# A seven-product block multiplication on TensorE: a new order of the products, a held queue of adding transfers, and operands in pieces of 512

## The chip, the cores and the metric

The kernel runs on one core of one Trainium2 chip. A core has TensorE (matrix products, written to the eight banks of PSUM), VectorE, ScalarE, GpSimd and SyncE, each with an instruction stream of its own that runs in order, and 16 DMA engines that all transfers share. In the profile these are PE, DVE, ACT, POOL and SP. The metric is the device time of one execution in microseconds (us), less being better.

## The reference, cut to what matters

One layer of a decoder trunk on 512 positions of 2048 channels, in float32:

```python
h = rmsnorm(x, norm_g)
proj = h @ w_in                      # 2048 x 15360
a_u, a_b, a_c, a_z, b_v, b_g, b_z, c_u, c_z, gates = split(proj)
y_a = short_conv_mixer(a_u, a_b, a_c, a_z, ...)      # 3 taps, then @ w_br_a
y_b = conformer_conv_mixer(b_v, b_g, b_z, ...)       # 31 taps, layer norm, then @ w_br_b
y_c = pool_mixer(c_u, c_z, ...)                      # causal means, then @ w_br_c
g = sigmoid(gates)                                    # 3 x 2048
merged = g0 * y_a + g1 * y_b + g2 * y_c
out = rmsnorm(x + merged @ w_o, final_g)
```

The change lies in the projection `h @ w_in`, 15360 columns wide.

## The kernel before, in words

**Units and products.** The projection is done in 15 units of 1024 columns (two column blocks of 512, "left" and "right"). In each unit the input x is cut into a 2 by 2 grid (256 positions by 1024 channels each), the weights into a 2 by 2 grid (1024 channels by 512 columns), and the block product is formed by seven products instead of eight, by sums and differences of the blocks (a Winograd form of Strassen's scheme). The seven are named in `PRODUCTS` (L58): 11, 12, s1, s4, s2, s3, 22. Each runs over 8 slices of 128 channels, in 4 steps of two slices.

**Halves.** Every operand of float32 is split in a high part (a cast by ACT) and a low part (a subtraction by DVE). A product takes three matmuls per slice and bank: high x high (L433), low x high (L434), high x low (L435). So a product is 8 slices x 2 banks x 3 = 48 matmuls of 512 columns, a unit 336.

**Weights.** `Weights` (L92) runs a list of stages, four per product (28 per unit). A stage's raw weights lie in a tile of 128x1024: rawA (4 buffers) or rawB (6). "load" is a transfer from SP's queue (L113); "add" is a transfer from POOL's queue that adds a second block to what lies in the tile (L119); "sum" is an addition on DVE of the tile that another product holds (L134). `split_to` (L144) then makes `wh` on ACT (L155) and `wl` on DVE (L156) in 3 buffers each, two stages ahead of the product. An add may start only when the split before it has read the tile.

**Banks.** In `unit` (L422) 11 is written to two banks X, 12 to two banks V, s1 to two banks Z, s4 into Z on top, s2 into X on top, s3 into X, 22 into X. Between two products into the same banks, their contents are copied out by ACT (`snap`, L441) or added to an earlier copy by DVE (`join`, L446), and the next product's first matmul must wait for that. `on11` to `on22` finish the four quarters (gates, SiLU and so on); in the first unit they are put off into the second one (`delayed`), since the norm's factor is not known yet.

**The first unit** also makes the seven operands of x, which stay for all later units: `make` (L365) scales by the norm's gain (`gcol`), forms sums and differences (`less`, L357) and splits them in halves (`operand`, L344, and `quarter`, L349). x11, x12, x22, x21 are read by SP's queue (L228), interleaved with the first weights.

**What sets the order.** Engine streams are laid down by a scheduler ahead of time, from the program's order and priorities; on the chip each stream runs in order. Between the matmuls `feed` hands out a list of side tasks (convolution taps, pooling, norms) at half a unit of cost per slice. After the units come three branch products and the output product, which the change doesn't touch.

Of the kernel before, what the change touches and what calls it, by code (L numbers as in the profile page):

```python
# [8 lines left out]
F32 = mybir.dt.float32  # L9
# [37 lines left out]
for _c in (0, CH):  # L47
# [8 lines left out]

PRODUCTS = (
    ("11", "A", "load", 0, 0),  # L58
    ("12", "B", "load", 1, 0),
    ("s1", "A", "add", 0, 1),  # L60
    ("s4", "B", "load", 1, 1),
    ("s2", "A", "sum", 1, 1),
    ("s3", "B", "add", 0, 1),
    ("22", "A", "add", 1, 0),
)
STEPS = KD // 4
# [13 lines left out]
def stages():  # L80

    out = []
    for u in range(len(UNITS)):
        for name, tag, what, row, col in PRODUCTS:
            key = (u, tag, name == "12")
            out += [(tag, key + (s,), what, block(u, row, col, s)) for s in range(STEPS)]
# [5 lines left out]
class Weights:  # L92
# [3 lines left out]
    def __init__(self, tc, nc, pools, parts, src, load_ahead, split_ahead):  # L96
# [4 lines left out]
        self.first_sum = {s[3]: n for n, s in enumerate(self.stages) if s[2] == "sum"}  # L101
        self.raw, self.raw_of, self.held, self.done = {}, {}, {}, {}
        self.loaded = self.summed = self.split = self.at = 0

    def load_to(self, n):
        while self.loaded < min(n, len(self.stages)):
            tag, key, what, b = self.stages[self.loaded]
            if what == "sum":
                pass
            elif what == "load":  # L110
                t = self.pools[tag].tile([P, RAW], F32, tag=tag, name=f"raw{tag}{self.loaded}")
                for at in self.pieces(self.loaded):
                    self.nc.sync.dma_start(out=t[:, at], in_=self.src[b][:, at])  # L113
            else:
                t, before = self.raw[key]
                assert self.split > before
                first = self.first_sum.get(self.raw_of[key], -1)
                assert first < self.summed
                self.nc.gpsimd.dma_start(out=t, in_=self.src[b], accum_op=ALU.add)  # L119
            if what == "load":  # L120
                self.raw_of[key] = b
                self.held[b] = t
            if what != "sum":
                self.raw[key] = t, self.loaded
            self.loaded += 1

    def sum_to(self, n):
        while self.summed < min(n, len(self.stages)):
            _, key, what, b = self.stages[self.summed]
            if what == "sum":  # L130
                t, before = self.raw[key]
                assert self.split > before and self.loaded > self.summed
                with self.tc.high_priority(AHEAD):
                    self.nc.vector.tensor_tensor(out=t, in0=t, in1=self.held[b], op=ALU.add)  # L134
                self.raw[key] = t, self.summed
# [908 lines left out]
```

## Time and profile before

| | |
|---|---|
| Median of 3 runs | 1708.18 us (1707.02 to 1710.57) |
| The profiled execution's own time | 1707.05 us |
| Its span (first to last instruction) | 1705.3 us |
| DVE busy | 1140.5 us (67%) |
| ACT busy | 736.4 us (43%) |
| Matmuls | 7332, weight loads for them 7332 |
| First product starts | 7.10 us |
| HBM read, written | 277.00 MB, 35.65 MB |

Busy time is the time in which an engine executes; a share that is high over the span says little of a stage. The profile names, for each idle stretch of an engine, what ended it ("PE X L433 <- DVE snap L446": the matmul into X on L433 waited for DVE's `join`). A matmul of 512 columns is listed with some 0.39 us, since its end is modelled; back to back they start every 0.23 us, so short delays show only in their starts.

### The profile page before, as it was taken

How to read it: one execution, taken by the hardware profiler on the slowest of the kernel's cores; microseconds unless marked ns; L12 is line 12 of the kernel's file. 1: busy time of each engine (PE TensorE's matmuls, PEld its weight loads, DVE VectorE, ACT ScalarE, POOL GpSimd, SP SyncE). 2: the span in 40 equal slices, each digit the busy share in tenths (PEclk: the TensorE clock that was granted, in tenths of full speed). 3: DMA queues.
4: the chain of work that ended last, by engine and by line, in shares of the span. 5: the costliest groups of instructions: out<-in, count | busy, mean ns of one | idle time of the engine just before them, and what ended most of it. 6: DMA issues, size and time to landing. Idle time of an engine off the chain costs nothing.

```text
span 1705.3 us, 19733 instructions
## 1 busy us (share of the span) xinstructions
PE 1651.0 (97%) x7332; PEld 1348.6 (79%) x7332; DVE 1140.5 (67%) x1420; ACT 736.4 (43%) x919; POOL 156.9 (9%) x186
## 2 busy tenths in 40 slices
PE   7899999999999999999999989999999999999997
PEld 5677877877878787888878868888888888888887
DVE  5946699799869969967786866555743444453342
ACT  5645543434344454546544544445631211222222
POOL 1101010101011111111111111110100000000000
PEclk9999999999999999999999999999999999999999
DMA  9686867667585877688979887868994544443202
GB/s 309 141 242 140 232 140 193 143 179 168 153 181 142 196 189 171 181 217 262 267 206 251 244 237 168 225 158 240 255 314 153 181 144 148 136 136 100 91 34 99
DMA packets 110864, 313.95 MB, mean 184 GB/s; under 512 B 12208, under 2 KB 16432, under 8 KB 110768
## 3 DMA queue, kind: packets, MB, share of 16 engines
q1 hardware_dynamic: 63392, 179.50, 31.7%
q0 software_dynamic: 25920, 94.38, 30.5%
q10 hardware_dynamic: 21456, 38.82, 6.2%
q8 instruction: 57, 0.93, 0.2%
q14 instruction: 39, 0.32, 0.1%
HBM read 277.00 MB, written 35.65 MB: 183 GB/s over the span
## 4 chain that ended last, share of the span: by engine, by line
PE 84%; DVE 6%; issue 2%; ACT 1%; DMA 1%; ACTq 0%; SPq 0%; DVEq 0%
PE X L433 11%; PE X L434 11%; PE X L435 11%; PE Z L433 5%; PE Z L435 5%; PE y L872 5%; PE y L870 5%; PE y L871 5%; PE Z L434 5%; PE o L944 3%; PE o L946 3%; PE o L945 3%; DVE wl L156 2%; PE V L433 2%; PE V L434 2%; PE V L435 2%
## 5 line engine op out<-in xcount | busy, mean ns | idle before, releaser
L156 DVE TENSOR_TENSOR wl<-rawA,wh 128x1024 fp32r<-128x1024 f32 (+1 forms) x281 | 342.1, 1219 | 219.2 <-ACT wh L155 216.6
L155 ACT CAST wh<-rawA 128x1024 fp32r<-128x1024 f32 (+1 forms) x281 | 294.5, 1050 | 448.6 <-PE X L434 133.3
L156 DVE TENSOR_TENSOR wl<-rawB,wh 128x1024 fp32r<-128x1024 f32 x220 | 268.4, 1223 | 256.3 <-ACT wh L155 256.2
L155 ACT CAST wh<-rawB 128x1024 fp32r<-128x1024 f32 x220 | 231.4, 1053 | 348.5 <-PE X L434 103.7
L433 PE MATMUL X<-wh,x 128*128 128x512 f32 x480 | 188.4, 395 | 17.7 <-DVE snap L446 14.8
L433 PE MATMUL Z<-wh,xs 128*128 128x512 f32 x480 | 188.8, 396 | 5.5 <-ACT snap L441 4.1
L433 PE MATMUL X<-wh,xs 128*128 128x512 f32 x480 | 189.3, 395 | 1.9 <-ACT xs L346 1.7
L434 PE MATMUL Z<-wh,xs 128*128 128x512 f32 x480 | 188.5, 393 | 2.0 <-DVE xs L347 2.0
L434 PE MATMUL X<-wh,x 128*128 128x512 f32 x480 | 188.2, 392 | 0.1
L434 PE MATMUL X<-wh,xs 128*128 128x512 f32 x480 | 187.5, 391 | 0.0
L435 PE MATMUL X<-wl,xs 128*128 128x512 f32 x480 | 174.1, 391 | 6.4 <-DVE wl L156 6.3
L435 PE MATMUL Z<-wl,xs 128*128 128x512 f32 x480 | 175.1, 395 | 5.1 <-DVE wl L156 5.1
L435 PE MATMUL X<-wl,x 128*128 128x512 f32 x480 | 177.5, 394 | 0.0
L556 DVE SCALAR_TENSOR_TENSOR conv<-v,prm,conv 128x485 f32<-128x485 f32 (+14 forms) x240 | 167.4, 732 | 0.1
L119 POOL DMA_DIRECT2D rawA<-wts x120 | 104.1, 868 | 567.0 <-DVE wl L156 553.3
L870 PE MATMUL y<-wh,u 128*128 128x512 f32 x384 | 149.9, 390 | 0.0
L871 PE MATMUL y<-wh,u 128*128 128x512 f32 x384 | 149.7, 390 | 0.0
L872 PE MATMUL y<-wl,u 128*128 128x512 f32 x384 | 149.5, 390 | 0.0
L433 PEld LDWEIGHTS X<-wh,x 128*128 128x128 f32 x480 | 90.4, 189 | 42.0 <-issue 10.2
L433 PEld LDWEIGHTS Z<-wh,xs 128*128 128x128 f32 x480 | 90.7, 189 | 30.8 <-ACT snap L441 10.2
L433 PEld LDWEIGHTS X<-wh,xs 128*128 128x128 f32 x480 | 90.3, 188 | 27.7 <-ACT snap L441 6.3
L435 PEld LDWEIGHTS Z<-wl,xs 128*128 128x128 f32 x480 | 90.1, 189 | 27.7 <-DVE wl L156 9.2
(173 smaller groups left out, 2360.2 us busy)
## 6 DMA issues: line engine op xcount, KB each, us to landing
rawB<-wts SPq DMA_DIRECT2D x160, 512.0 KB, 5.2
rawA<-wts POOLq DMA_DIRECT2D x120, 512.0 KB, 8.1
rawA<-wts SPq DMA_DIRECT2D x99, 512.0 KB, 4.2
rawB<-wts POOLq DMA_DIRECT2D x60, 512.0 KB, 6.0
g<-g SPq DMA_DIRECT2D x48, 256.0 KB, 4.3
d<-turn ACTq DMA_DIRECT2D x32, 256.0 KB, 7.7
g<-gate ACTq DMA_DIRECT2D x24, 256.0 KB, 4.1
g<-snap ACTq DMA_DIRECT2D x24, 256.0 KB, 5.4
```

Of the source, the lines that this page charges most:

```text
L119: self.nc.gpsimd.dma_start(out=t, in_=self.src[b], accum_op=ALU.add)
L155: self.nc.scalar.copy(out=h[:, at], in_=raw[:, at])
L156: self.nc.vector.tensor_tensor(out=l[:, at], in0=raw[:, at], in1=h[:, at].bitcast(F32), op=ALU.subtract)
L433: T.matmul(p, lhsT=xh, rhs=h, start=start and k == 0, stop=False, skip_group_check=True)
L434: T.matmul(p, lhsT=xl, rhs=h, start=False, stop=False, skip_group_check=True)
L435: T.matmul(p, lhsT=xh, rhs=l, start=False, stop=k == KB - 1, skip_group_check=True)
L556: V.scalar_tensor_tensor(out=c[:, s:], in0=v[:, : S - s], scalar=pcol(P_BW, i * CONV_B + CONV_B - 1 - s), in1=c[:, s:], op0=ALU.mult, op1= ...
L870: T.matmul(banks[t], lhsT=uh[:, tk], rhs=h, start=k == 0, stop=False)
L871: T.matmul(banks[t], lhsT=ul[:, tk], rhs=h, start=False, stop=False)
L872: T.matmul(banks[t], lhsT=uh[:, tk], rhs=l, start=False, stop=k == KB - 1)
L944: T.matmul(pt[t], lhsT=mh[:, tk], rhs=h, start=k == 0, stop=False)
L945: T.matmul(pt[t], lhsT=ml[:, tk], rhs=h, start=False, stop=False)
```

## The change

- The products' order in every unit but the first becomes 11, s1, s2, s4, s3, 12, 22, so that between two products into the same pair of banks there is one into another pair. Since s2's sum needs the block of s4 before s4 runs, that block is loaded earlier.
- In the first unit the order is 11, 12, s1, s2, s4, s3, 22, and s2's weights come by an adding transfer in place of the DVE sum.
- The transfers are planned ahead as a list of events. An add is issued one stage after the split that frees it at the earliest; s1 and s3 now follow their predecessor in the tile (11 and s4) by four stages, where it was eight.
- POOL gets a copy of one column, `hold`, which reads the last block of x12; POOL's later transfers stand behind it.
- The operands: scaling by ACT in two pieces of 256 in place, then the cast and the subtraction on 512 at once; sums and differences on 512 too. `ngcol` goes.

```diff
 PRODUCTS = (
     ("11", "A", "load", 0, 0),
+    ("s1", "A", "add", 0, 1),
+    ("s2", "A", "sum", 1, 1),
+    ("s4", "B", "load", 1, 1),
+    ("s3", "B", "add", 0, 1),
     ("12", "B", "load", 1, 0),
...
     ("22", "A", "add", 1, 0),
 )
+FIRST = (PRODUCTS[0], PRODUCTS[5], PRODUCTS[1], ("s2", "A", "add", 1, 1), *PRODUCTS[3:5], PRODUCTS[6])
...
+        for n, (_, key, what, b) in enumerate(self.stages):
             if what == "load":
-                self.raw_of[key] = b
-                self.held[b] = t
+                out.append((min(need[b], n) - self.load_ahead, n))
+            elif what == "add":
+                out.append((max(n - self.load_ahead, before[key] + 1), n))
+            before[key] = n
+        return sorted(out)
...
+    def transfer(self):
+        n = self.events.popleft()[1]
+        tag, key, what, b = self.stages[n]
+        if what == "load":
+            t = self.raw[key] = self.held[b] = self.pools[tag].tile([P, RAW], F32, tag=tag, name=f"raw{tag}{n}")
+            for at in self.pieces(n):
+                self.nc.sync.dma_start(out=t[:, at], in_=self.src[b][:, at])
+        else:
+            self.nc.gpsimd.dma_start(out=self.raw[key], in_=self.src[b], accum_op=ALU.add)
...
-            self.load_to(n_stage + 1)
-            self.sum_to(n_stage + 3)
-            self.load_to(n_stage + 1 + self.load_ahead)
+            self.sum_to(n_stage + 2)
+            while self.events and self.events[0][0] <= n_stage:
+                self.transfer()
...
     for j in range(STEPS):
-        w.load_to(STEPS + j + 1)
+        w.transfer()
         xload(nc.sync, x12[j], j, 1, 0)
+    hold = const.tile([P, 1], F32, name="hold")
+    nc.gpsimd.tensor_copy(out=hold, in_=x12[STEPS - 1][:, 1, HT - 1 :])
...
-    def quarter(name, j, src, rows):
-        t = sets[name][j] = slot(F32R, f"x{name}")
+    def scale(src, j, rows):
+
         for c in range(2):
-            g = gcol[:, KB * rows + 2 * j + c :][:, :1]
-            h, l = t[:, c, half[0]], t[:, c, half[1]]
-            A.activation(out=h, in_=src[:, c], func=AF.Copy, scale=g)
-            V.scalar_tensor_tensor(
-                out=l, in0=src[:, c], scalar=g, in1=h.bitcast(F32), op0=ALU.mult, op1=ALU.subtract
-            )
...
+            A.activation(out=src[:, c], in_=src[:, c], func=AF.Copy, scale=gcol[:, KB * rows + 2 * j + c :][:, :1])
+
+    def less(out, in0, in1, sign=None):
+
+        if sign is None:
+            V.tensor_tensor(out=out, in0=in0, in1=in1, op=ALU.subtract)
+        else:
+            V.scalar_tensor_tensor(out=out, in0=in0, scalar=sign, in1=in1, op0=ALU.mult, op1=ALU.subtract)
...
         if name == "11":
-            quarter(name, j, x11, 0)
+            scale(x11, j, 0)
+            operand(name, j, x11)
         elif name == "12":
-            quarter(name, j, x12[j], 1)
+            scale(x12[j], j, 1)
+            operand(name, j, x12[j])
         elif name == "s1":
...
-            less(qs[j], x22[j], x21, j, 1, gcol)
+            scale(x21, j, 0)
+            scale(x22[j], j, 1)
+            less(qs[j], x22[j], x21)
+            operand(name, j, qs[j])
+        elif name == "s2":
+            less(qs[j], x11, qs[j], -1.0)
             operand(name, j, qs[j])
         elif name == "s4":
-            less(qs[j], x11, qs[j], j, 0, ngcol)
-            less(x12[j], x12[j], qs[j], j, 1, ngcol)
-            operand(name, j, x12[j])
-        elif name == "s2":
+            less(qs[j], qs[j], x12[j], -1.0)
             operand(name, j, qs[j])
...
         X = [psum("X") for _ in range(2)]
         run("11", X, True)
         a = snap(X)
-        U = [psum("V") for _ in range(2)]
-        run("12", U, True)
-        join(U, a, on11)
+        if first:
+            second()
         Z = [psum("Z") for _ in range(2)]
         run("s1", Z, True)
         e = snap(Z)
-        run("s4", Z, False)
         run("s2", X, False)
         u = snap(X)
+        run("s4", Z, False)
         join(Z, u, on12)
         run("s3", X, False)
         join(X, e, lambda i, t: on22(i + 2, t))
+        if not first:
+            second()
         run("22", X, False)
```

The new `second()` runs 12 and joins its banks. In `multiplied` the product of the left and right quarter is now formed when both are there, since 12 may come last.

PE's stream in the second unit, before: the last matmuls of s3 and the first of 22, all into the banks X_870 and X_871.

```order
L433 MATMUL X_871<-wh_1300,xs_60_704 128x512
L434 MATMUL X_871<-wh_1300,xs_60_704 128x512
L435 MATMUL X_871<-wl_1301,xs_60_704 128x512
L433 MATMUL X_870<-wh_1318,x_61_724 128x512
L434 MATMUL X_870<-wh_1318,x_61_724 128x512
```

PE's stream in the second unit of the changed kernel, where s3 (into X_851 and X_852) ends and 12 (into V_1264 and V_1265) begins.

```order
L434 MATMUL X_852<-wh_1210,xs_60_696 128x512
L435 MATMUL X_852<-wh_1210,xs_60_696 128x512
L436 MATMUL X_852<-wl_1211,xs_60_696 128x512
L434 MATMUL V_1264<-wh_1227,x_21_233 128x512
L435 MATMUL V_1264<-wh_1227,x_21_233 128x512
L434 MATMUL V_1265<-wh_1227,x_21_233 128x512
```

48 matmuls of product 12 now stand between s3 and 22; in the same way s2 stands between s1 and s4, and s4 between s2 and s3. In the first unit s3 and 22 still follow each other.

POOL's stream at the start, before: the adds of s1 (onto 11's tiles rawA_93 to rawA_103), then those of s3.

```order
L242 AFFINE_SELECT ident<-ident 128x128
L119 DMA rawA_93<-wts 128x1024
L119 DMA rawA_97<-wts 128x1024
L119 DMA rawA_100<-wts 128x1024
L119 DMA rawA_103<-wts 128x1024
L119 DMA rawB_334<-wts 128x1024
```

POOL's stream at the start of the changed kernel; x_8_88 is the last block of x12.

```order
L249 AFFINE_SELECT ident<-ident 128x128
L132 DMA rawA_93<-wts 128x1024
L132 DMA rawA_97<-wts 128x1024
L132 DMA rawA_100<-wts 128x1024
L132 DMA rawA_103<-wts 128x1024
L242 COPY hold<-x_8_88 128x1
L132 DMA rawA_93<-wts 128x1024
```

The copy stands behind the four adds of s1 and ahead of the adds of s2, which are new.

ACT's stream in the first unit, before: from the split of s1's first weights (wh_336) to the first operand of s1 (xs_30_331).

```order
L155 CAST wh_336<-rawA_93 128x1024
L376 ACTIVATE xa_81<-xa_81,gcol 128x256
L155 CAST wh_362<-rawA_97 128x1024
L376 ACTIVATE xa_81<-xa_81,gcol 128x256
L376 ACTIVATE xa_82<-xa_82,gcol 128x256 x2
L155 CAST wh_392<-rawA_100 128x1024
L346 CAST xs_30_331<-q_326 128x2x256
```

The same stretch of the changed kernel (wh_337 to xs_30_332; x_9 to x_11 are blocks of x22, x_28_306 is the last operand of 12).

```order
L160 CAST wh_337<-rawA_93 128x1024
L357 ACTIVATE x_9_89<-x_9_89,gcol 128x256 x2
L351 CAST x_28_306<-x_8_88 128x2x256
L357 ACTIVATE xa_81<-xa_81,gcol 128x256 x2
L357 ACTIVATE x_10_90<-x_10_90,gcol 128x256 x2
L357 ACTIVATE xa_82<-xa_82,gcol 128x256 x2
L357 ACTIVATE x_11_91<-x_11_91,gcol 128x256
L160 CAST wh_365<-rawA_97 128x1024
L357 ACTIVATE x_11_91<-x_11_91,gcol 128x256
L351 CAST xs_30_332<-q_326 128x2x256
```

Ahead of the first operand of s1 stand the scalings of x22 and a cast for 12, which were not there; one weight cast (of rawA_100) moved behind it.

## Rows read from the trace of the kernel before

**Rows 1.** The page: span, and busy time of each engine.

```profile
span 1705.3 us, 19733 instructions
PE 1651.0 (97%) x7332; PEld 1348.6 (79%) x7332; DVE 1140.5 (67%) x1420; ACT 736.4 (43%) x919; POOL 156.9 (9%) x186
```

**Rows 2.** PE's waits from 100 to 1290 us: in total, times, longest.

```profile
PE X L433 <- DVE snap L446: 12.4, 13, 2.4
PE X L435 <- DVE wl L156: 6.3, 2, 4.2
...
PE Z L433 <- ACT snap L441: 3.1, 3, 1.4
```

**Rows 3.** PE's timeline, 11 to 12: start, duration, engine, line, operation, tiles.

```profile
1109.26 0.39 PE L435 MATMUL X<-wl,x 128*128 128x512 f32 x1
1109.49 0.39 PE L433 MATMUL V<-wh,x 128*128 128x512 f32 x1
```

**Rows 4.** PE's timeline where s1 ends and s4 begins in the same banks.

```profile
1131.02 0.39 PE L435 MATMUL Z<-wl,xs 128*128 128x512 f32 x1
1131.41 0.50 PE L433 MATMUL Z<-wh,xs 128*128 128x512 f32 x1
1131.75 0.40 PE L434 MATMUL Z<-wh,xs 128*128 128x512 f32 x1
```

**Rows 5.** Units: length, busy PE, PEld, DVE, ACT, POOL; PEclk, DMA share, GB/s.

```profile
343.87:425.46 81.59, 79.42 (x353) 64.34 (x353) 81.59 (x104) 33.59 (x36) 10.38 (x12) 1.00 0.70 171
506.96:589.22 82.26, 80.50 (x353) 65.68 (x353) 80.13 (x101) 36.21 (x41) 10.41 (x12) 0.98 0.69 167
753.37:835.50 82.13, 81.93 (x372) 66.78 (x373) 61.09 (x66) 50.29 (x65) 10.38 (x12) 1.00 0.93 258
1087.65:1164.91 77.26, 77.07 (x336) 62.82 (x337) 42.71 (x39) 37.44 (x43) 10.42 (x12) 1.00 0.77 191
```

**Rows 6.** PE's timeline in the first unit: 12's first matmuls and 22's first.

```profile
25.66 1.22 PE L433 MATMUL V<-wh,x 128*128 128x512 f32 x2 [5.78 <-ACT x L354]
...
98.72 0.47 PE L433 MATMUL X<-wh,x 128*128 128x512 f32 x1 [2.32 <-DVE snap L446]
```

**Rows 7.** Stretches of 5 us in the first unit, columns as in rows 5.

```profile
20.00:25.00 5.00, 0.00 (x0) 0.00 (x0) 1.23 (x1) 1.04 (x1) 0.00 (x0) 0.76 1.05 254
...
45.00:50.00 5.00, 5.00 (x20) 4.07 (x19) 5.00 (x11) 2.09 (x3) 0.00 (x0) 0.85 0.41 151
...
75.00:80.00 5.00, 5.00 (x24) 4.14 (x23) 5.00 (x10) 3.23 (x5) 1.73 (x2) 1.00 0.77 129
```

**Rows 8.** DVE's timeline in the first unit.

```profile
44.26 1.67 DVE L362 SCALAR_TENSOR_TENSOR q<-xa,ngcol,q 128x256 f32<-128x256 f32 x4
...
46.44 1.22 DVE L134 TENSOR_TENSOR rawA<-rawA,rawB 128x1024 f32<-128x1024 f32 x1
47.58 0.48 DVE L362 SCALAR_TENSOR_TENSOR x<-x,ngcol,q 128x256 f32<-128x256 f32 x1
...
68.73 2.50 DVE L347 TENSOR_TENSOR xs<-q,xs 128x512 fp32r<-128x512 f32 x4
```

**Rows 9.** ACT's timeline in the first unit.

```profile
20.09 1.04 ACT L155 CAST wh<-rawB 128x1024 fp32r<-128x1024 f32 x1 [2.96 <-DMA rawB<-wts]
25.10 0.91 ACT L354 ACTIVATE x<-x,gcol 128x256 fp32r<-128x256 f32 x2 [3.96 <-DMA x<-xT]
...
39.39 0.61 ACT L346 CAST xs<-q 128x512 fp32r<-128x512 f32 x1
39.91 0.91 ACT L376 ACTIVATE xa<-xa,gcol 128x256 f32<-128x256 f32 x2
```

**Rows 10.** POOL's timeline: the first adds of s1 in the first and in a later unit.

```profile
6.48 1.01 POOL L119 DMA_DIRECT2D rawA<-wts  x1 [5.10 <-DVE wl L156]
...
1095.75 0.86 POOL L119 DMA_DIRECT2D rawA<-wts  x1 [24.39 <-DVE wl L156]
```

**Rows 11.** The adding transfers of L119: issue to landing.

```profile
DMA to landing us min/median/max: 5.3/7.1/12.7
```

**Rows 12.** The page's DMA queues: packets, MB, share of 16 engines' span.

```profile
q0 software_dynamic: 25920, 94.38, 30.5%
```

More of the change, by code (lines that the diff above doesn't have):

```diff
@@ L100, in __init__ @@
         self.last = {s[1]: n for n, s in enumerate(self.stages)}
[L101 to L107, printed above, removed]
-            if what == "sum":
[L109 to L113, printed above, removed]
-            else:
[L115 to L119, printed above, removed]
-            if what == "load":
-                self.raw_of[key] = b
-                self.held[b] = t
-            if what != "sum":
-                self.raw[key] = t, self.loaded
-            self.loaded += 1
@@ new lines, in __init__, with plan @@
+        self.raw, self.held, self.done = {}, {}, {}
+        self.events = deque(self.plan())
+        self.summed = self.split = self.at = 0
+    def plan(self):
+        need, before, out = {}, {}, []
+        for n, (_, key, what, b) in enumerate(self.stages):
+            if what == "sum":
+                need[b] = n - 2
+            else:
+                need.setdefault(b, n)
+        for n, (_, key, what, b) in enumerate(self.stages):
+            if what == "load":
+                out.append((min(need[b], n) - self.load_ahead, n))
[3 more added lines that the diff above has]
+        return sorted(out)
@@ L130, in sum_to @@
             if what == "sum":
[L131 to L132 removed]
+                t = self.raw[key]
                 with self.tc.high_priority(AHEAD):
                     self.nc.vector.tensor_tensor(out=t, in0=t, in1=self.held[b], op=ALU.add)
[L135 removed]
             self.summed += 1
@@ L244, in trunk @@
     )
-    ngcol = const.tile([P, KD], F32, name="ngcol")
-    V.tensor_scalar(out=ngcol, in0=gcol, scalar1=-1.0, scalar2=None, op0=ALU.mult)
     ones = const.tile([P, P], F32, name="ones")
@@ L417, in roots, with unit @@
         V.tensor_tensor(out=R2n, in0=Rp, in1=Rn, op=ALU.mult)
-    def unit(on11, on12, on21, on22, each=lambda n: None):
+    def unit(on11, on12, on21, on22, each=lambda n: None, first=False):
         n = [0]
@@ L447, in join, with second @@
                 then(i, t)
+        def second():
+            U = [psum("V") for _ in range(2)]
+            run("12", U, True)
+            join(U, a, on11)
         X = [psum("X") for _ in range(2)]
@@ L479, in multiplied, with product, on11 @@
         L, Rr, got = [None] * NT, [None] * NT, [None] * NT
+        def product(t):
+            if L[t] is not None and Rr[t] is not None:
+                times(L[t], L[t], col(r, t), Rr[t])
+                got[t] = L[t]
+        def on11(t, x):
+            L[t] = x
+            product(t)
         def on12(t, x):
-            times(L[t], L[t], col(r, t), right(t, x))
-            got[t] = L[t]
+            Rr[t] = right(t, x)
+            product(t)
         def on21(t, src):
@@ L800, in trunk @@
             if n == 0:
-                unit(**delayed(hooks), each=first_each)
+                unit(**delayed(hooks), each=first_each, first=True)
             else:
```

26 lines of the change are left out of this document (7 added, 19 removed).

## The prediction

> **What bounds the kernel now.** I read the page first: PE is busy for 1651.0 of 1705.3 us [rows 1], so nothing but PE's own idle time, some 54 us, and matmuls that start late can be won. Next the list of PE's waits, for the stretch of the units after the first. The reader is to see two names that come again and again: 13 waits of a matmul into X for DVE's join, 12.4 us, and 3 waits of a matmul into Z for ACT's snap, 3.1 us [rows 2]. They stand where a product goes into banks that the product before it has just left, 22 after s3 and s4 after s1. The third entry, two waits for a low half of weights, 6.3 us, is another thing. Then PE's timeline at two hand-overs, since a short delay has no idle entry. From 11 to 12, which have banks of their own, the starts are 0.23 us apart as everywhere [rows 3]. From s1 to s4 in the same banks they are 0.39 and 0.34 us apart [rows 4], a delay of 0.16 + 0.11 = 0.27 us. Last the first unit by itself: PE waits 5.78 us for the first block of x12 and 2.32 us at its 22 [rows 6], and DVE has no idle time in any of the seven stretches of 5 us from 45 to 80 us (the first and the last of them in [rows 7]). So later units are bound by PE with short holes, the first one by transfers up to 25 us and by DVE from 45 to 80 us.
>
> **Part 1, the order of the products in units 2 to 15.** PE keeps its instructions. Every wait between products of the same banks gets a product of 48 x 0.23 = 11.0 us in front of it, and the longest of them lasted 2.4 us [rows 2], so these waits go. Shown waits: 12.4 + 3.1 = 15.5 us [rows 2]. Not shown: two hand-overs a unit (s1 to s4, s2 to s3) in 14 units, less the 3 shown, 25 x 0.27 = 6.8 us [rows 4]. Together 22.3 us. What is late next:
> - In the unit from 343.87 us DVE is busy for 81.59 of 81.59 us [rows 5]. A unit can't be shorter than DVE's work in it; the wait for the join there is DVE's lateness, and it would come back as a wait for a low half. I take off a mean wait and two hand-overs, 12.4/13 + 0.54 = 1.5 us. The unit from 506.96 us has 82.26 - 80.13 = 2.1 us of room, which is enough.
> - In the units from 753 to 1010 us DMA is busy for 0.93 of the time in the first [rows 5], and the two waits for low halves of rows 2 lie near their end. I count nothing won in these three: 3 x 1.5 = 4.5 us off.
> That leaves 22.3 - 1.5 - 4.5 = 16.3, rounded 16 us. Bounds: 22 us, if nothing comes back; 5 us, if DVE gives back three quarters.
>
> **Part 2, the shorter lead of the adds.** s1's add waits for the split of 11 and s3's for that of s4, as before, but only four stages later the tile is wanted, not eight. In the trace the first add of s1 of a unit is issued at 1095.75 us [rows 10]; that unit's 11 starts 48 matmuls after 1087.65 us [rows 5], at 1098.7, and s1 would now start 11.0 us later, at 1109.7. So there are 14.0 us from issue to use. ACT's cast of the weights takes 1.04 us [rows 9], so the transfer may take 12.9 us. It takes 7.1 us in the middle and 12.7 at most [rows 11]. I cost it at nothing; the cover is the two stages by which splits run ahead, and it is thin in the stretch where DMA is nearly full. Behind a late cast on ACT stand the snaps and gates, and DVE's low half.
> The load of the block that s2's sum shares with s4 moves forward, at no cost: SP's stream has it a unit ahead.
>
> **Part 3, the first unit.**
> - The copy `hold` costs nothing and wins nothing. In POOL's stream it stands behind s1's four adds, so these still go out from 6.48 us on [rows 10], among the transfers of x12, and PE still waits until about 25 us. What stands behind it, the adds of s2, needs s1's low halves anyway, which come later than the last block of x12.
> - 11's last step gets later: its cast stands behind the cast of rawB, which runs at 20.09 us when that has landed [rows 9]. PE's idle stretch before 12 ends only when x12 lands at 25.10 us [rows 9], so this is hidden. With the cast added to the scaling, 12 starts some 0.8 us later.
> - ACT on the way to s1's first operand (now cast at 39.39 us): four casts of 512 for 12 at 39.91 - 39.39 = 0.52, and five scalings of 256 at 0.41 (0.91 us a pair) [rows 9], 4.1 us; one weight cast of about 0.95 goes behind, and some 2.4 us were idle. So s1 starts about 0.8 us later.
> - DVE in its full stretch loses the four sums, 47.58 - 46.44 = 1.14 each, 4.6 us. 40 pieces of 256 at 1.67/4 = 0.42 become 20 of 512 at 2.50/4 = 0.63 [rows 8]: 16.8 - 12.6 = 4.2 us. Together 8.8 us less work in a stretch that DVE bounds, less the 0.8 us of later start: 8.0. Not all of it reaches PE, since some low halves of weights now stand behind operand pieces at the start of s2; I take 7 us. Bounds: 0 (PE then waits for transfers instead) and 11 (its waits and half-rate stretches between 40 and 70 us gone too).
> - The four added adds: q0's 30.5% of 1705.3 us over 180 adds is 2.9 us of all engines each [rows 1, 12], 11.6 us, in a stretch whose DMA share falls to 0.41 [rows 7]. No cost.
> - The wait of 2.32 us at 22 [rows 6] stays: in the first unit 22 still follows s3.
>
> The Trainium skill (DMA: Bandwidth & Descriptors, section SWDGE vs HWDGE vs iDMA) says that each DMA engine takes turns between the queues of the two kinds of issuers. By that rule s1's adds take their full turn from x12, and holding them back would pay. The order of POOL's stream shows that they aren't held.
>
> **The sum.** 1707.05 - 16 - 7 = 1684.05 us for an execution like the profiled one. The median of the runs is 1708.18, 1.13 above it, so 1685 us.
>
> **The rivals.**
> - *The freed time goes into waits for low halves.* For it: DVE is full in one unit and near it in another [rows 5], and the sums of s2 stand among s1's low halves. Against it: from 1087.65 us on DVE is at 42.71 of 77.26 us. Then part 1 is worth 6 and part 3 gives 3: 1708.2 - 9 = 1699 us. Chance 0.18.
> - *More goes than I count.* The two long waits for low halves (6.3 us) vanish with the new order of transfers, nothing is given back (22 instead of 16), and the first unit gives 10: 1708.2 - 22 - 6 - 10 = 1670 us. The case that the adds of s1 are held after all, which would take away 5.78 us [rows 6], ends near it. Chance 0.14.
> - *Slower: the adds come too late.* One mechanism, at s3's adds, which go out right behind 22's adds and so land last in a run of eight. It decides from a landing time of 12.9 us on, and the longest is 12.7 [rows 11]; with fewer holes in PE the run gets denser. A wait of 6.3/2 = 3.15 us (the mean of the two for low halves) in 14 units is 44 us, against 23 won: 1708.2 - 23 + 44 = 1729 us; in half the units 1707, no change. For it: the maximum touches the limit. Against it: the middle lies at 7.1. Chance 0.08, half of that in between.
>
> **How the numbers follow.** My forecast has 0.60, with its own range of 1676 to 1694 us. Least and most of the parts: 5 + 0 and 22 + 11 us, 1703 and 1675 us. The range of eight in ten reaches from 1670 (the second rival) to 1702. A measurement of this kernel tells some 0.2%, 3.4 us, from no change. Faster by more than that: 0.60 + 0.17 + 0.13 = 0.90, within it 0.04, slower 0.06.
>
> **What would show it.** In the profile after: no waits of X for DVE's join or of Z for ACT's snap in units 2 to 15, the one at 22 of the first unit still there; units of gates 0.5 us or more below 77.26; the idle stretch before 12 still ending after 25 us; s1's start near 41 us; DVE full from there but done with the first unit's operands about 8 us earlier; the second unit starting some 7 us earlier. Wrong would be: many waits of PE on ACT's `wh` in s1 or s3 behind an add (then the lead decided), the units from 344 and 507 us no shorter, or the hole before 12 gone.

## The result, and the profile after

| | before | changed |
|---|---|---|
| median of 4 runs each, us | 1709.38 (1707.02 to 1711.29) | 1667.43 (1665.61 to 1667.68) |
| profiled execution, us | 1707.05 | 1667.63 |
| its span, us | 1705.3 | 1665.8 |
| ratio of times, 95% interval | | 0.9753 (0.9736 to 0.977) |

The kernel became 42 us faster; 23 were forecast, and 1667 lies below the range of 1670 to 1702. Three executions further down, of e4, of e9 and of the kernel before, took over 2100 us and are in no ratio. All the difference is in PE's time. The page of the changed kernel, answering to [rows 1]:

```profile
span 1665.8 us, 19674 instructions
PE 1633.9 (98%) x7332; PEld 1347.9 (81%) x7332; DVE 1131.3 (68%) x1387; ACT 740.9 (44%) x931; POOL 160.4 (10%) x191
```

PE's idle time fell from 54.3 to 31.9 us, and its busy time by 17.1 us with the same 7332 matmuls: matmuls start closer together, which no list of waits shows. Where the time went is read from two stretches between the same points, the 22 of the first unit and the 22 of the last. Before, with two of the units heavy in DMA below it (columns as in [rows 5]):

```profile
98.72:1242.39 1143.67, 1118.49 (x4949) 910.36 (x4949) 875.60 (x1033) 557.84 (x659) 145.75 (x168) 1.00 0.78 199
...
835.50:921.99 86.49, 85.04 (x372) 69.77 (x373) 65.83 (x99) 44.09 (x54) 10.41 (x12) 1.00 0.86 229
921.99:1010.36 88.37, 81.29 (x349) 65.94 (x348) 67.40 (x92) 42.33 (x50) 10.53 (x12) 0.98 0.86 241
```

The changed kernel, the same stretch and then single units (the one from 331.00 us answers to that from 343.87 in [rows 5], 487.15 to 506.96, 727.20 to 753.37, the next two to the rows just shown, 1050.50 to 1087.65):

```profile
94.74:1202.82 1108.08, 1103.77 (x4949) 911.35 (x4949) 875.79 (x1032) 556.81 (x660) 145.32 (x168) 1.00 0.81 205
331.00:409.00 78.00, 78.00 (x353) 64.67 (x352) 76.47 (x95) 32.44 (x35) 10.38 (x12) 1.00 0.74 176
...
487.15:565.50 78.35, 78.30 (x353) 64.60 (x352) 76.43 (x95) 34.84 (x39) 10.37 (x12) 1.00 0.73 171
727.20:809.10 81.90, 81.14 (x374) 67.00 (x373) 60.99 (x66) 49.76 (x65) 10.39 (x12) 1.00 0.93 256
809.10:890.70 81.60, 81.60 (x362) 67.57 (x361) 62.63 (x93) 41.86 (x51) 10.37 (x12) 1.00 0.89 232
890.70:974.30 83.60, 82.16 (x361) 67.40 (x360) 67.09 (x92) 43.05 (x51) 10.40 (x12) 1.00 0.94 264
1050.50:1126.66 76.16, 76.16 (x338) 63.06 (x336) 43.18 (x39) 37.41 (x43) 10.39 (x12) 1.00 0.81 193
```

Up to the first unit's 22 the change won 98.72 - 94.74 = 4.0 us, between the two 22s 1143.67 - 1108.08 = 35.6 us, behind that nothing (462.9 against 463.0). Of the 35.6, 20.9 us were idle time of PE (25.2 to 4.3) and 14.7 us busy time. DVE does the same work in both stretches, 875.60 and 875.79 us.

PE's waits in that stretch of the changed kernel (columns: engine, what it waited for, us, times, longest):

```profile
PE X L436 <- DVE wl L161: 3.4, 5, 1.0
PE X L434 <- ACT wh L160: 0.8, 1, 0.8
PE X L434 <- DVE snap L447: 0.2, 1, 0.2
```

Against [rows 2], the waits for join and snap are gone: the 0.2 us is the wait of the first unit's 22, with which this stretch begins. The waits for low halves (`wl`) went from 9.6 to 3.4 us: the list of before had one more entry, which stands here.

```profile
PE Z L435 <- DVE wl L156: 3.3, 6, 0.8
```

Now the hand-over that answers to [rows 4], s1 to s2 in the changed kernel's unit of gates. The starts are 0.23, 0.23 and 0.22 us apart, where they were 0.39 and 0.34:

```profile
1082.91 0.39 PE L436 MATMUL Z<-wl,xs 128*128 128x512 f32 x1
1083.14 0.39 PE L434 MATMUL X<-wh,xs 128*128 128x512 f32 x1
1083.37 0.39 PE L435 MATMUL X<-wh,xs 128*128 128x512 f32 x1
1083.59 0.39 PE L434 MATMUL X<-wh,xs 128*128 128x512 f32 x1
```

The first unit, answering to [rows 6]: the last step of 11, the start of 12, the start of s3 and the start of 22.

```profile
22.56 0.73 PE L434 MATMUL X<-wh,x 128*128 128x512 f32 x2 [2.19 <-ACT x L351]
...
27.04 0.73 PE L434 MATMUL V<-wh,x 128*128 128x512 f32 x2 [0.57 <-ACT x L351]
...
80.07 0.80 PE L434 MATMUL X<-wh,xs 128*128 128x512 f32 x1 [3.84 <-ACT wh L160]
...
94.74 0.47 PE L434 MATMUL X<-wh,x 128*128 128x512 f32 x1 [0.20 <-DVE snap L447]
```

The hole ahead of 12 has moved into 11, and a new one of 3.84 us stands at s3's weights. The stretch from 75 us, answering to the last of [rows 7], has PE and DVE nearly idle and DMA full:

```profile
75.00:80.00 5.00, 1.24 (x6) 0.69 (x4) 0.00 (x0) 1.02 (x2) 0.10 (x1) 0.98 1.07 215
```

POOL issues eight adds from 57 to 75 us: first the four of 22 (into rawA), behind them the four of s3 (into rawB). In the kernel before, s3's went out ahead of 22's, from 57.85 us on; now s4 runs after s2, so its tile comes free later. The eight take longer to land than the 7.1 us in the middle of [rows 11]. Below stand their landing times, the issue of s3's first add and the cast by ACT that waits for it:

```profile
DMA to landing us min/median/max: 7.4/11.3/12.8
```

```profile
67.66 0.86 POOL L132 DMA_DIRECT2D rawB<-wts  x1 [2.68 <-DVE wl L161]
```

```profile
78.97 1.04 ACT L160 CAST wh<-rawB 128x1024 fp32r<-128x1024 f32 x1 [6.59 <-DMA rawB<-wts]
```

### The profile page after: what moved, and what is told of

The parts are those of the page before. It is cut to its first block, busy times and chain, and to the rows that moved or that the text cites. A ratio compares the mean times of both kernels' runs of the same rounds, so it can differ in the third digit from the quotient of the medians.

```text
span 1665.8 us, 19674 instructions
## 1 busy us (share of the span) xinstructions
PE 1633.9 (98%) x7332; PEld 1347.9 (81%) x7332; DVE 1131.3 (68%) x1387; ACT 740.9 (44%) x931; POOL 160.4 (10%) x191
## 4 chain that ended last, share of the span: by engine, by line
PE 87%; issue 6%; DMA 3%; DVE 2%; POOL 1%; ACT 1%; SPq 0%; ACTq 0%; POOLq 0%; DVEq 0%
PE X L436 12%; PE X L434 12%; PE X L435 11%; PE y L888 5%; PE y L887 5%; PE y L886 5%; PE Z L436 5%; PE Z L434 5%; PE Z L435 5%; PE V L435 3%; PE V L434 3%; PE V L436 3%; PE o L961 3%; PE o L960 3%; PE o L962 3%
## 5 line engine op out<-in xcount | busy, mean ns | idle before, releaser
L436 PE MATMUL X<-wl,xs 128*128 128x512 f32 x480 | 168.8, 391 | 5.8 <-DVE wl L161 5.8
L436 PE MATMUL X<-wl,x 128*128 128x512 f32 x480 | 172.6, 394 | 0.0
L436 PE MATMUL Z<-wl,xs 128*128 128x512 f32 x480 | 169.9, 391 | 0.0
L572 DVE SCALAR_TENSOR_TENSOR conv<-v,prm,conv 128x511 f32<-128x511 f32 (+14 forms) x240 | 168.5, 727 | 0.0
L434 PEld LDWEIGHTS X<-wh,x 128*128 128x128 f32 x480 | 90.2, 189 | 27.3 <-ACT x L351 7.8
L436 PEld LDWEIGHTS X<-wl,xs 128*128 128x128 f32 x480 | 89.6, 188 | 26.7 <-DVE wl L161 8.3
L435 PEld LDWEIGHTS X<-wh,x 128*128 128x128 f32 x480 | 90.5, 189 | 20.9 <-DVE x L352 2.3
```

Source lines behind the costliest of these rows:

```text
L434: T.matmul(p, lhsT=xh, rhs=h, start=start and k == 0, stop=False, skip_group_check=True)
L435: T.matmul(p, lhsT=xl, rhs=h, start=False, stop=False, skip_group_check=True)
L436: T.matmul(p, lhsT=xh, rhs=l, start=False, stop=k == KB - 1, skip_group_check=True)
L572: V.scalar_tensor_tensor(out=c[:, s:], in0=v[:, : S - s], scalar=pcol(P_BW, i * CONV_B + CONV_B - 1 - s), in1=c[:, s:], op0=ALU.mult, op1= ...
```

## The experiments

Ratios are to runs of the kernel before, taken beside them on the same chip. Taken again later, the changed kernel itself had 1671.81 us and 0.9779 (e15), so 4 us between runs that were not taken side by side are no finding.

### Which part won it: the order alone (e1), the first unit (e4)

e1 puts the old order back in units 2 to 15 (in this list and in `unit`) and keeps everything else of the change; e4 does the reverse (old first unit, operands and sum, no `hold`).

```diff
 PRODUCTS = (                      # e1
     ("11", "A", "load", 0, 0),
+    ("12", "B", "load", 1, 0),
     ("s1", "A", "add", 0, 1),
-    ("s2", "A", "sum", 1, 1),
     ("s4", "B", "load", 1, 1),
+    ("s2", "A", "sum", 1, 1),
     ("s3", "B", "add", 0, 1),
-    ("12", "B", "load", 1, 0),
     ("22", "A", "add", 1, 0),
```

> The changed kernel, with the old order of products (11, 12, s1, s4, s2, s3, 22) in units 2 to 15; the first unit, its operands and the plan of transfers stay changed. Theory A (the order alone carries what the later units won, 35.6 us between the 22 of the first unit and the 22 of the last): 1667 + 35 = 1702 us, within 4, with X waits on DVE's join and long waits on low halves between 920 and 1010 us back, and units of gates at 77.26 us. Theory B (the order is worth the 16 us that I forecast, the other 20 come from the new plan of transfers with its shorter lead, which took the long waits for low halves away): 1667 + 16 = 1683 us, with no wait for a low half over 1 us between 920 and 1010 us.

> The changed kernel, with the first unit as before (order 11, 12, s1, s4, s2, s3, 22, DVE's sum for s2, operands in pieces of 256, no copy hold); units 2 to 15 and the plan of transfers stay changed. Theory A (the first unit won what the traces show at the start of its 22, 4.0 us): 1667 + 4 = 1671.5 us. Theory B (the first unit won the 7 us that I forecast, and lost 3 of them to the late adds of s3 alone): 22 starts again near 98.7 us, and the time is 1671.5 us too, but with the old adds under the new lead of three stages the wait before s3 comes back and 22 starts after 99 us.

e1: 1703.63 us, 0.9963 (0.9949 to 0.9977). Its stretch between the 22s, the unit with the long waits and a unit of gates:

```profile
94.38:1238.89 1144.51, 1120.63 (x4949) 911.37 (x4949) 875.56 (x1033) 558.53 (x660) 145.44 (x168) 1.00 0.77 198
918.10:1005.26 87.16, 81.55 (x350) 66.07 (x348) 67.40 (x92) 42.60 (x51) 10.45 (x12) 0.98 0.87 245
1084.15:1161.41 77.26, 77.07 (x336) 62.82 (x337) 42.70 (x39) 37.42 (x43) 10.40 (x12) 1.00 0.78 191
```

1144.51 us is the kernel before (1143.67) to within a microsecond, and the unit of gates has its 77.26 us back. Theory A holds: the new order carries all 36 us, and the list of events without it wins nothing. One thing e1 doesn't separate: the plan derives an add's place from the order, so the shorter lead of the adds went back with it.

e4: 0.9803 (0.9782 to 0.9824); three times from 1673.01 to 1680.08 us, too far apart to price the first unit. 22 starts at 97.82 us, 3.1 us later than in the changed kernel, where theory B wanted it after 99 us; B's other sign, a long wait ahead of s3, isn't there either: with the old order s3's adds go out from 57.57 us on.

### What one hand-over costs (e2, e3)

e2 orders 11, 12, s1, s2, s4, s3, 22 (only s3 to 22 in the same banks), e3 orders 11, s1, s4, s2, s3, 12, 22 (the two others).

> The changed kernel, with product 12 second again in units 2 to 15 (11, 12, s1, s2, s4, s3, 22): of the three hand-overs in the same banks only s3 to 22 is back. Theory A (what a hand-over costs is its wait, shown or not, and nothing is given back): the 13 shown waits of 12.4 us and some 0.3 us beside each of the 14, 1667 + 16.5 = 1683.5 us. Theory B (DVE's lateness is what counts in the full units, and comes back elsewhere whatever the order): 1667 + 10 = 1677 us or less, with the units of 78 us (from 331 and 487 us in the changed kernel) no longer than they are.

> The changed kernel, with s1, s4, s2, s3 back to back again in units 2 to 15 (11, s1, s4, s2, s3, 12, 22): the hand-overs s1 to s4 and s2 to s3 are back, 12 still stands ahead of 22. Theory A: 28 hand-overs of 0.3 to 0.45 us and the rest of the 3 shown waits, 3.1 - 3 x 0.36 us: 1667 + 12 = 1679 us. Theory B (a hand-over without a shown wait costs the 0.27 us that I read between matmul starts, or less): 1667 + 28 x 0.27 + 2 = 1676.5 us or below. In a unit of gates, where no wait is shown, A says 76.16 + 0.7 us or more, B 76.16 + 0.54 or less.

e2: 1697.00 us, 0.9922 (0.9907 to 0.9937). e3: 1689.77 us, 0.9878 (0.9862 to 0.9894). Both lie above both of their theories. The unit of gates, which has no long wait, is the clean measure; e2, then e3:

```profile
1080.56:1157.17 76.61, 76.41 (x337) 62.99 (x337) 42.74 (x39) 37.33 (x43) 10.39 (x12) 1.00 0.79 192
```

```profile
1074.54:1151.37 76.83, 76.83 (x338) 62.91 (x336) 43.19 (x39) 37.52 (x43) 10.40 (x12) 1.00 0.81 192
```

Above 76.16 us: s3 to 22 costs 0.45 us, of which the trace shows 0.20 as idle; the two others cost 0.67 us together, 0.335 each, none of it shown (theory A said 0.7 or more, B 0.54 or less: it lies between, close to A). 0.45 + 0.67 = 1.12 is the whole of 77.26 - 76.16 = 1.10 us. Over 14 units this is 6.3 us in e2 and 9.4 in e3. The rest of the two results is longer waits in the earlier units, and slow matmuls behind them: 18.4 us in 14 waits for the join in e2 (13.9 in e1), and in e3 the waits below.

```profile
PE Z L442 <- ACT snap L450: 8.5, 3, 4.2
PE Z L444 <- DVE wl L169: 4.1, 2, 2.9
PE X L444 <- DVE wl L169: 3.1, 1, 3.1
```

A long wait can cost more than its length. Behind the longest one of e2 the matmuls start 0.43 us apart instead of 0.23; 12 of them in a row do so, 12 x 0.2 = 2.4 us on top of 3.42. The granted clock of that stretch is 0.50, the lower of its two levels, 1.2 GHz. Not every wait does it: behind one of 2.17 us in the kernel before, at 982.35 us, they start 0.23 us apart.

```profile
261.24:266.36 5.12, 5.12 (x13) 3.96 (x12) 5.12 (x8) 0.00 (x0) 0.00 (x0) 0.50 0.48 166
```

```profile
260.68 0.77 PE L442 MATMUL X<-wh,x 128*128 128x512 f32 x1 [3.42 <-DVE snap L455]
```

So the prices of the hand-overs add up only where nobody is late; a half-repaired order has waits of its own. Why these waits are longer, up to 4.2 us for the snap of e3, was not followed further.

### Why the long waits for low halves went (e9, e13)

In the kernel before PE waits 4.17 us for a low half:

```profile
1006.19 1.22 PE L435 MATMUL X<-wl,xs 128*128 128x512 f32 x2 [4.17 <-DVE wl L156]
```

ACT's cast, which makes the high half that DVE needs for it, and then DVE's stream:

```profile
997.30 1.05 ACT L155 CAST wh<-rawB 128x1024 fp32r<-128x1024 f32 x1
```

```profile
1001.45 0.69 DVE L627 TENSOR_TENSOR c<-c,rstd 128x512 f32<-128x512 f32 x1 [5.17 <-DMA c<-cd]
...
1004.92 1.22 DVE L156 TENSOR_TENSOR wl<-rawB,wh 128x1024 fp32r<-128x1024 f32 x1
```

DVE stood 5.17 us at a product whose operand was still being fetched, with the low half behind it. On SP that fill (a spilled block of c, read back) went out behind two weight loads:

```profile
989.37 3.05 SPq L113 DMA_DIRECT2D rawB<-wts  x2
992.48 1.22 SPq L214 DMA_DIRECT2D c<-cd  x1
```

e9 lets ACT issue the fills of c and z; e13 leaves out the last block of c.

```diff
-        held[i] = fill(cd[i], "c")                 # e9: on ACT's queue, z likewise
+        held[i] = fill(cd[i], "c", nc.scalar)
```

```diff
-            before(load, i)                        # e13: for the last i only
-            add(2.6, act, i)
+            add(2.6, lambda: (ubd.__setitem__(KB - 1, ubd[KB - 2]), rstd.clear()))
```

> The kernel before, with one edit: the fills of c and z (spilled blocks of the convolution) are issued by ACT instead of SP. It is about the two waits of PE for low halves at 982.35 and 1006.19 us, 6.3 us, that went with the new order. Theory A (a chain of queues: SP stands 11.6 us at a weight load that needs a free buffer of rawB, the fill of c behind it goes out only at 992.48 us, DVE stands 5.2 us at the sum that needs it, and the low halves stand behind that): the fills land in time, DVE has no wait for c over 2 us in that unit, the two waits are under 2 us together, 1709 - 5 = 1704 us. Theory B (the transfers are late since DMA is busy for 0.86 of the time there, whatever queue they stand in): the waits stay at 5 us or more, 1709 us.

> The kernel before, with the last of the eight blocks of c left out (its two fills, four operations of DVE and one of ACT; the block before it is used in its place). It takes away the fill that DVE stood 5.17 us for, ahead of the low half that PE then waited 4.17 us for at 1006.19 us. Theory A (DVE's stream, in order, with low halves behind a sum that waits for a fill; the issuing queue doesn't matter, as the run with the fills on ACT showed): the wait at 1006 us goes below 0.5 us, that at 982 us (2.17 us, behind shorter waits for other fills) stays, 1709 - 5 = 1704 us. Theory B (the low halves there are late because their weights are late, DMA being busy for 0.86 of the time): the wait stays at 3 us or more, 1709 us less at most 1.

e9: 1712.70 us, 1.0023 (1.0012 to 1.0033), no gain. The fill is as late, and DVE stands as long. But the edit didn't move the moment of issue: on ACT's queue the fill goes out at 998.00 us, 0.58 us behind the start of the same weight load (997.42), where it was 0.39 us on SP. ACT had just waited 1.17 us to copy the banks out. So e9 doesn't show whether a place in a queue holds the fill back, and theory B's busy transfers stay possible:

```profile
998.00 0.33 ACTq L214 DMA_DIRECT2D c<-cd  x1
```

```profile
1006.15 0.69 DVE L627 TENSOR_TENSOR c<-c,rstd 128x512 f32<-128x512 f32 x1 [4.92 <-DMA c<-cd]
```

e13: 1702.68 us, 0.996 (0.9945 to 0.9975). The wait at 1006 us is gone; what is left at that place is the join:

```profile
1004.95 0.47 PE L433 MATMUL X<-wh,x 128*128 128x512 f32 x1 [0.67 <-DVE snap L446]
```

The unit from 923.38 to 1004.95 us takes 81.57 us instead of 88.37. (Between the first 22 and the last, e13 gains only 3.4 us: its second and third unit are 3.1 us longer, which this edit doesn't explain.) The cast at 997.30 us says the same: the late low half stood in DVE's stream behind a fill, its weights were there. e13 also takes away DVE's work on that block, so the 6.8 us are not the fill's alone. The wait of 2.17 us at 982.35 us should have stayed; 1.22 us of it are left. With the new order DVE's waits for c are shorter (in total, times, longest, from 727 to 985 us; 8.2 us in three waits in the kernel before), and that unit takes 83.60 us:

```profile
DVE c L643 <- DMA c<-cd: 3.7, 2, 2.4
```

What sets the late issue of that fill (992.48 us), and why it comes earlier with the new order, stays open: neither its place in a queue nor a buffer that is not yet free was excluded.

### The first unit (e5 to e8)

e5 makes its operands in pieces of 256 again; e6 leaves `hold` out; e8 makes s2 by DVE's sum; e7 makes the hold real:

```diff
-    nc.gpsimd.tensor_copy(out=hold, in_=x12[STEPS - 1][:, 1, HT - 1 :])
+    for j in range(STEPS):
+        nc.gpsimd.tensor_tensor(
+            out=hold[:, j : j + 1], in0=x12[STEPS - 1][:, 1, HT - 1 :],
+            in1=w.raw[0, "A", False, j][:, RAW - 1 :], op=ALU.add)
```

> The changed kernel, with the first unit's operands made in pieces of 256 again (its order of products, its adds and hold stay). Theory A (the first unit is bound by DVE from s1 on, as I forecast): DVE's 4.2 us of shorter pieces come back, 22 starts near 98.5 us instead of 94.74, time 1667 + 4 = 1671 us. Theory B (the adds of s3 set the end of the first unit, PE waits 3.84 us for one at 80.07 us, and DVE's lighter work is hidden behind that wait): 22 starts within 0.8 us of 94.74, time 1667 to 1668 us, with the wait shorter by what DVE is later.

> The changed kernel without the copy hold. Theory A (it stands behind s1's four adds and holds only s2's, which need s1's low halves anyway): no change, 1667.4 us within 1.5, 22 starts within 0.8 us of 94.74. Theory B (the copy does delay something that pays): s2's adds go out ahead of 36 us and 12 starts later than 27.5 us, time over 1669 us.

> The changed kernel with the hold made real: four tiny sums on POOL read the last block of x12 and a column of each of 11's weight tiles, so that s1's adds can't go out before that block has landed. Theory A (the adds take their share from x12's transfers, and that is what PE waits for): x12's first block lands 4 us or more before 25.4 us, 12 starts by 24 us, and s1's adds land in time; the time is 1663 us. Theory B (what 12 wins is lost again, since s1 waits for x21, x22 and their scalings until 41 us whatever 12 does): 12 starts earlier, 22 starts within 1 us of 94.74, 1667 us. Theory C: the adds now land after 41 us and s1 starts later, 1670 us or more.

> The changed kernel, with s2 of the first unit made by DVE's sum again instead of four adding transfers. Theory A (the four adds of s2 push those of s3 back, and that is the wait of 3.84 us; DVE's four sums cost 4.6 us where DVE is full): the wait before s3's weights goes, DVE takes 0.8 us more than it gave, 22 starts at 95 to 96 us, 1668 us. Theory B (DVE isn't what the first unit waits for): 22 starts at 91 us, 1664 us. Theory C (DVE sets it alone): 22 starts at 99 us, 1672 us.

- e5: 1670.78 us, 0.978 (0.9753 to 0.9807). 12 starts at 25.25 us and 22 at 92.27, 2.5 us *earlier* than with pieces of 512. Theory A falls, and B, for which 22 should have stayed: the pieces of 512 won nothing in the first unit. The profiled execution isn't shorter, though (1669.59 us): its third unit is 3.9 us longer (85.55 against 81.69), with a wait of DVE that comes back in e15.
- e6: 1668.71 us, 0.9771 (0.9744 to 0.9798), 22 at 95.69 us. 12 starts at 30.24 us, a sign of theory B, but not by B's mechanism: s2's adds go out at 38.45 us, not ahead of 36. The copy holds back nothing.
- e8: 1669.37 us, 0.9771 (0.9747 to 0.9795), 22 at 94.89 us. These are the numbers of its theory A, but its mechanism isn't there: without s2's adds s3's first add goes out later, at 69.40 instead of 67.66 us, and ACT can cast that block at 79.40 instead of 78.97 us. PE's waits shrink from 3.84 to 0.66 and 1.00 us because PE comes to s3 later. In both kernels s3 starts 1.1 us after the start of that cast, and 22 some 14.5 us after s3: the first unit's end hangs on s3's first add. What makes PE later in e8 is not separated: 12 starts at 29.81 us, and DVE has four sums more.
- e7: 1663.92 us, 0.9739 (0.9716 to 0.9762). The four loads of x12, from issue to landing, in the changed kernel and then in e7:

```profile
DMA to landing us min/median/max: 14.5/18.0/18.5
```

```profile
DMA to landing us min/median/max: 8.1/8.1/8.2
```

PE's rows of e7, at the starts of 12, s1 and 22:

```profile
21.48 0.62 PE L445 MATMUL V<-wh,x 128*128 128x512 f32 x2
37.22 0.79 PE L445 MATMUL Z<-wh,xs 128*128 128x512 f32 x1 [4.71 <-ACT wh L168]
...
89.94 0.47 PE L445 MATMUL X<-wh,x 128*128 128x512 f32 x1 [0.77 <-DVE snap L458]
```

12 starts 5.6 us earlier without a wait. s1's adds, now late, cost 4.71 us at 37.22 us, and 22 still starts 4.8 us earlier: theory A in 12 and in the time, with C's price inside it.

### A better version (e10, e11, e12, e14, e15, e16)

e10 adds pieces of 256 for 11 to the real hold, e14 for all operands; in e11 step j's add waits for x12's block j instead of the last (`x12[j]` in e7's edit), e12 is e11 with e10's pieces; e15 is the changed kernel and e16 e7, once more on one chip.

> The changed kernel with the real hold (s1's adds wait for x12's last block) and 11's operands made in pieces of 256 straight from x11 again (the scaling of x11 for s2 and s3 comes later, on ACT). Theory A (pieces of 512 make 11 late at its start and its last step, as the starts of 12 at 25.25 us with pieces of 256 and 27 to 30 us with 512 show; the first unit passes that on): 12 starts by 20.5 us, 22 by 89 us, 1663 us. Theory B (s1 waits for its adds, which start at x12's last block whatever 11 does): 22 starts at 90 us, 1664 us, as with the real hold alone.

> The changed kernel with a looser hold: the add of s1's step j waits for block j of x12 instead of for the last one. Theory A (with the real hold PE waits 4.71 us for s1's first weights, so earlier adds help, and x12's first block is what 12 waits for): 12 starts at 22 us, s1's wait is under 2 us, 22 starts at 88 us, 1662 us. Theory B (the first adds take the share of x12's later blocks, 12 is late inside): 22 starts at 90 to 92 us, 1664 to 1666 us.

> Both: the looser hold and 11's operands in pieces of 256. If each gains what its theory A says, 12 starts by 21 us, 22 by 87.5 us and the time is 1660 to 1661 us; if the adds of s1 set the first unit, it equals the looser hold alone.

> The changed kernel with the real hold and all operands of the first unit in pieces of 256 again. Theory A (DVE no longer bounds the first unit, which was not full after 55 us with the real hold): 22 starts within 1 us of the 89.94 us of the real hold alone, 1664 us. Theory B (DVE's 4.2 us of longer pieces come through): 22 starts at 93 us or later, 1667 us.

> The changed kernel itself once more, as the measure for the next run on the same chip: 1667.4 us within 1.5.

> The changed kernel with the real hold, once more beside the changed kernel on the same chip. If the real hold wins what its first run showed (22 of the first unit 4.8 us earlier), it is 3 to 5 us below the changed kernel, with intervals that do not overlap; if that was the spread from run to run, within 1.5 us of it.

| | us | ratio | 12 starts | 22 starts |
|---|---|---|---|---|
| e10 | 1664.77 | 0.9743 (0.9722 to 0.9764) | 20.88 | 89.35 |
| e11 | 1671.50 | 0.978 (0.9761 to 0.9799) | 19.81 | 95.29 |
| e12 | 1674.77 | 0.9801 (0.9779 to 0.9823) | 20.06 | 96.18 |
| e14 | 1663.32 | 0.9729 (0.9712 to 0.9746) | 19.44 | 88.61 |
| e15 | 1671.81 | 0.9779 (0.9762 to 0.9796) | 26.77 | 93.58 |
| e16 | 1665.93 | 0.9743 (0.9727 to 0.9758) | 21.72 | 90.21 |

Side by side on one chip the real hold is 5.9 us below the changed kernel, times apart (1663.62 to 1667.86 against 1669.94 to 1672.85). In the profiled executions 3.4 us of it are there at the first unit's 22; as much again is the longer third unit of e15, below. e14, with the old pieces, has the lowest median, but its interval overlaps that of e16: behind a real hold the pieces don't matter much (theory A, though 22 starts 1.3 us before e7's, not within 1 us). e10 lies with its theory B. e11 and e12 miss in the other direction. In e11 x12's blocks land early (the last at 22.57 us), but the adds now run beside the loads of x22 and x21. ACT stands at the scaling of x22's first block, which lands at 28.12 us, and the cast for 12's last step comes behind it in ACT's order; PE waits 6.98 us for that at 35.11 us.

```profile
28.14 0.91 ACT L368 ACTIVATE x<-x,gcol 128x256 f32<-128x256 f32 x2 [4.27 <-DMA x<-xT]
...
34.46 0.60 ACT L362 CAST x<-x 128x512 fp32r<-128x512 f32 x1
```

e15 also shows one source of the spread between runs of the changed kernel. 22 of its first unit starts 1.2 us earlier than in the first profile, yet its third unit is 4.6 us longer (86.33 against 81.69), with a wait of 3.81 us for a low half. DVE's and PE's rows there:

```profile
200.34 0.55 DVE L565 TENSOR_SCALAR conv<-v,prm 128x512 f32<-128x512 f32 x1 [3.99 <-DMA v<-d]
...
201.46 1.22 DVE L161 TENSOR_TENSOR wl<-rawA,wh 128x1024 fp32r<-128x1024 f32 x1
```

```profile
202.73 0.98 PE L436 MATMUL Z<-wl,xs 128*128 128x512 f32 x2 [3.81 <-DVE wl L161]
```

It is the mechanism of e13 at another place: a fill that lands late, DVE in order, a low half behind. The first profile of the changed kernel has no wait of DVE for v there; e5 and e8 have one, of 3.1 and 3.3 us.

## Why the prediction was wrong, point by point

**The step that failed is the sum of part 1**, 16 us where the chip gave 35.6; e1 shows that they go with the order. The mechanism, a product between two in the same banks, was right; three terms were not: the hand-overs without a shown wait were mis-sized, the waits for low halves were put at nothing, and the 6 us taken off for what would come back were not lost. By its terms:

| term of part 1, us | forecast | measured |
|---|---|---|
| waits shown for join and snap [rows 2] | 15.5 | 15.5 |
| hand-overs without a shown wait | 6.8 | 14.7 (all of the busy time) |
| waits for low halves, less one on ACT | 0 | 9.6 - 3.4 - 0.8 = 5.4 |
| given back in the unit full of DVE | -1.5 | none |
| nothing won in three DMA-heavy units | -4.5 | none |
| sum | 16.3 | 35.6, as by the windows |

- *"Not shown: two hand-overs a unit ... 25 x 0.27 = 6.8 us."* I compared the first two starts behind a hand-over and stopped there, and I took the third hand-over, s3 to 22, as paid by its shown wait. e2 and e3 give 0.335 us twice and 0.25 us beside the shown part: 0.92 a unit, 12.9 us in 14 if the price of the quiet unit holds in all of them. The number stood in the trace of before. Its product 12, the one without a hand-over on either side, starts at 1109.49 us [rows 3] and the next product here:

```profile
1120.37 0.39 PE L433 MATMUL Z<-wh,xs 128*128 128x512 f32 x1
```

That is 10.88 us a product, seven are 76.16, and the quiet unit's 77.26 us [rows 5] are 1.10 above it; I had rounded the product to 11.0 us. The remaining 14.7 - 12.9 = 1.8 us fit half-rate stretches behind long waits: two units of before had a clock of 0.98, the one from 506.96 in [rows 5] and the one from 921.99, at most 0.02 x (82.26 + 88.37) = 3.4 us, and none of those shown after has.
- *"I count nothing won in these three."* They won (82.13 + 86.49 + 88.37) - (81.90 + 81.60 + 83.60) = 9.9 us by the windows of both kernels. I took a DMA share of 0.93 [rows 5] for a limit. It rose to 0.94 in a unit that became shorter; e13 shows that the longer of the two waits was the low half's place in DVE's line.
- *"A unit can't be shorter than DVE's work in it."* True, and of no use: DVE's 81.59 us were not that unit's work. In the changed kernel the unit takes 78.00 us with 76.47 of DVE, while DVE's work in the whole stretch is the same.

**Part 2** (0 us) is right for units 2 to 15: 0.8 us of waiting for a cast in all of them. In the first unit the wait of 3.84 us stands at s3's weights, which is the place, the mechanism (s3's adds behind 22's) and the size (3.15) that the slower rival gave. It decided once, not 14 times, and without a landing time of 12.9 us: 11.3 us (78.97 - 67.66) were enough, since there only 8.6 us lay between the add's issue and the moment at which PE stood ready (80.07 - 3.84 - 67.66).

**Part 3**, 7 us, measured 4.0. It looked at DVE's work and not at s3's adds, on whose landing the end of the first unit now hangs. Of its points:
- `hold` does nothing: right (e6). The sentence on the Trainium skill (DMA: Bandwidth & Descriptors, section SWDGE vs HWDGE vs iDMA), that engines take turns between the queues, agrees with e7: with s1's adds away, x12 lands in 8.1 us instead of 18.0, and holding them does pay. The price that the second rival gave it, 5.78 us, was near the 4.8 us that e7 won.
- "12 starts some 0.8 us later": it was 1.4, for another reason. PE doesn't wait for x12 but inside 11, whose last step comes behind a cast on ACT; e5 takes that back.
- DVE's 8.8 us less work: there (DVE has no work from 75 to 80 us), but worth nothing by itself. e5 had 22 earlier with the old pieces of 256. A stretch in which DVE has no idle time is not yet bound by its work, if its order is set by what arrives.
- "The four added adds ... No cost": not refuted. The wait of 3.84 us isn't theirs, since e8 leaves them out and s3's first block lands no earlier. What was missed is that s3's adds moved from 57.85 to 67.66 us.
- The wait of 2.32 us at 22 should have stayed; it is 0.20, probably since s3's own wait gave DVE time (DVE is idle from 75 to 80 us); no run shows it by itself.

**Rivals.** The nearest was the second, "more goes than I count", 1670 us at 0.14, with 28 us in units 2 to 15 and 10 in the first; measured were 35.6 and 4.0. The first rival, low halves taking the freed time, didn't come: PE's waits for them fell from 9.6 to 3.4 us, and even in e2 and e3 they are 3.7 and 7.2 us.

## What to carry to other kernels

Measure a hand-over by a whole quiet unit against its matmuls at the pitch of an undisturbed run, not by the first gaps that catch the eye; here a hand-over into a bank that is still being read cost 0.34 to 0.45 us even where nobody was late, most of it in no list of waits. The rule is the one of the Trainium skill (Perfetto Trace Analysis, section Matmuls), to rotate independent groups of matmuls through different banks; the 76.16 us of a quiet unit agree with it. And before calling a wait for an operand "late data", read the in-order stream of the engine that makes it: what stands at its head may have nothing to do with the operand. A hold works only if what it shall hold depends on it.

## What had not been expected

- A half-repaired order costs more than its share: e2 and e3 lose 29 and 21 us by their ratios (0.9922 and 0.9878 against 0.9753), together more than the 36 us of e1, which has all three hand-overs.
- One late fill of 256 KB (128x512 in f32) costs a unit of this kernel 4 us and more through DVE's order: 86.33 - 81.69 = 4.6 us in e15, and 88.37 - 81.57 = 6.8 us in the unit of before where e13 leaves out the fill and DVE's work on it.
- The end of the first unit hangs on s3's adds, which the change moved by 10 us: with s4 after s2 they go out behind 22's. Whether their old place ahead of 22's would win back the 3.84 us, no run here shows.
